# DeltaNet solves in a hybrid decoder trunk: heads stepped by one beat every second row tile, with their matmuls held between two of a projection, and the last residual's transposes held behind one

## The chip, the core and the metric

The kernel runs on one core of a Trainium2 chip. Its engines work side by side, each through its own instructions in the order written for it: TensorE (PE; its weight loads are listed as PEld), VectorE (DVE), ScalarE (ACT), GpSimd (POOL) and SyncE (SP), which here issues most of the transfers. They wait for each other through semaphores. The metric is the device time of one launch in microseconds.

## What is computed

Two decoder layers over 256 tokens of width 2048, all in float32: layer 0 mixes with sparse attention and retention, layer 1 with a gated DeltaNet; each layer then has a cross-attention into 256 memory tokens and a SwiGLU network. The change touches the DeltaNet mixer and the last residual. Cut to what matters:

```python
def gated_deltanet_mixer(h, w_in, conv_w, a_log, dt_bias, norm_gain, w_out):
    qkv, z, b, a = jnp.split(h @ w_in, cuts, axis=-1)
    qkv = jax.nn.silu(causal_depthwise_conv(qkv, conv_w))
    q, k, v = ...                       # 16 query/key heads, 32 value heads of 128
    o = chunk_gated_delta_rule(l2(q), l2(k), v, sigmoid(b), g)
    o = rms_norm(o, norm_gain) * jax.nn.silu(z)
    return o @ w_out

def chunk_gated_delta_rule(q, k, v, beta, g):          # chunks of 64 tokens
    lower = strict(kb @ k.T * decay)
    u, w  = triangular_solve(I + lower, [v * beta, kb * exp(gc)])
    # scan over the chunks:
    v_new = u - w @ state
    o = (q * exp(gc)) @ state + causal(q @ k.T * decay) @ v_new
    state = state * last + k_dec.T @ v_new
```

## The kernel before

Every projection runs as three float32r passes over a high and a low part of its operands (`passes`, L228). A weight tile comes by a SP transfer (L221), ACT makes its high part `w_hi` (L214), DVE the low part `w_lo` (L215), and PE multiplies it into a PSUM tile `pj` (L237, 256 columns a matmul).

Everything else is written as generators ("tasks"). `passes`' callers call `tick()` every six such matmuls, which advances each task that is due; `yield 1` in a task means two ticks, so twelve projection matmuls. This fixes the order in which the program is recorded; a scheduler then fixes the order on each engine, from its own model of durations, and may let instructions pass one another. A held instruction (`tc.issue_after(x)`) may not pass `x`.

In the DeltaNet mixer the sequence is: key and value projections; `invert`, which builds the inverses of all chunk matrices in a tile `AB` and writes them to DRAM as `d_T` by four stores issued from ACT (L1362); the last group of query projections, `queries(3)`; then for g = 0 to 7 a value projection and the solves of four heads, and last the output projection of `o`. A query group is convolved (`cv`: ACT L1061, then three DVE instructions L1063 for each 128 channels), passed through SiLU (`dq`, ACT L1067), and for each of its four heads turned (PE L386), squared and summed (`junk`, ACT L389), scored against the keys (`qk`, PE L1071 and L1072) and copied out (`R`, ACT L1254).

A solve (`pair`, L1394, for two heads; `head`, L1417, for one) takes a PSUM bank of the four in `psg`; the query heads use the same four. `pair` loads blocks of inverses `bd` (L1404) and a row of decays `gb` (L1410). The pool of these tiles lies on the memory of `AB`, so they wait until the four stores have landed. `head` then makes

- `M` and `At`: three DVE instructions (L1422 to L1424, from `gb`), an ACT exponential (L1425), two DVE products (L1426, L1427);
- the value head turned by two PE transposes (L1437) and scaled out as `bv` by two ACT copies (L1441);
- matmuls L1444 and ACT copy `nT` (L1446), then for the two row tiles L1455, DVE L1456, L1458, ACT copy `u` (L1459), with L1452 and DVE L1453 between the tiles;
- the outputs, L1461 to L1463, their sums of squares on ACT (L1467), two POOL instructions (L1468, L1469), three on DVE (L1470, L1472 twice, into `nT`);
- two transposes of `nT` (L1477), and the ACT copy into `R` (L1481) that frees the bank for the next head.

Each head is a task of its own and steps on when it is due; the pace between its steps is `HOP`. The value projection of group g starts when the heads of group g-2 have been turned (`turned`). ACT later splits `o` from `R` (L1013, with DVE and POOL L1014).

## Time and profile before

| | before |
|---|---|
| median of 3 runs | 3003.91 us (3001.68 to 3008.66) |
| the profiled run | 3001.64 us |
| its span in the trace | 2999.8 us, mean granted clock of PE 0.997 |
| PE busy | 2957.6 us, 99% of the span |
| DVE, ACT, POOL busy | 2033.3, 1703.5, 110.3 us |
| solves in the trace | about 1754 to 2077 us |

The span is the traced part; the run is 1.8 us longer. "Busy" of PE counts a matmul from its start to a modelled end, and successive matmuls overlap. PEclk is the share of full speed (2.4 GHz) that PE's clock was granted, 0.5 being 1.2 GHz. An idle time in square brackets stands before its instruction, with the engine and line that ended it. Two transposes or one matmul of 128 columns in plain float32 make two records.

### The profile page before, as it was taken

Reading aid. Unit: us, or ns where it says so; the run is one execution under the profiler, and the core shown is the slowest. Engines: PE = TensorE matmul, PEld = TensorE weight load, DVE = VectorE, ACT = ScalarE, POOL = GpSimd, SP = SyncE. Lnnn points to the kernel's source line nnn. Section 1 sums busy time; section 2 is a strip of 40 time slices with the busy share of each in tenths; the row PEclk is TensorE's granted clock in tenths of the full one; section 3 lists DMA queues with packets and bytes.
Section 4 is the critical chain, followed back from the end, with each engine's and each line's share of the span. In section 5 each row is a group of like instructions: output and inputs, shape, how many; then the busy total and the mean of one; then the engine's idle time right before and its main releaser. Section 6 shows DMA issues by size and latency. Waiting matters only on the chain.

```text
span 2999.8 us, 59557 instructions
## 1 busy us (share of the span) xinstructions
PE 2957.6 (99%) x22917; PEld 2830.7 (94%) x22917; DVE 2033.3 (68%) x3879; ACT 1703.5 (57%) x3328; POOL 110.3 (4%) x153
## 2 busy tenths in 40 slices
PE   8999999999999999999999989999999999999999
PEld 8989899999999999999978989999999999999887
DVE  6867676776665665557689978886667656655554
ACT  6655655665555554447665657776556555445444
POOL 0000000000000000000110101121000000000000
PEclk9999999999999999999999999999999999999999
DMA  7776555656666665566677676663656666666665
GB/s 237 203 233 178 156 147 176 186 174 195 193 195 193 195 195 193 196 191 187 185 220 230 178 208 178 176 177 127 194 187 182 191 193 194 184 189 183 197 199 166
DMA packets 327641, 566.97 MB, mean 189 GB/s; under 512 B 41868, under 2 KB 71620, under 8 KB 327100
## 3 DMA queue, kind: packets, MB, share of 16 engines
q1 hardware_dynamic: 321280, 545.02, 61.0%
q10 hardware_dynamic: 3500, 10.33, 1.3%
q0 software_dynamic: 2576, 7.82, 0.9%
q8 instruction: 179, 2.93, 0.4%
q14 instruction: 106, 0.87, 0.1%
HBM read 549.16 MB, written 13.93 MB: 188 GB/s over the span
## 4 chain that ended last, share of the span: by engine, by line
PE 94%; DMA 2%; DVE 2%; ACT 1%; issue 1%; POOL 0%; SPq 0%; ACTq 0%; DVEq 0%; POOLq 0%
PE pj L237 87%; DVE w_lo L215 1%; DMA w<-in_hyb_w_in 1%; DMA d_T<-AB 1%; PE slv L1458 0%; PE slv L1455 0%; PE slv L1444 0%; ACT w_hi L214 0%; DMA w<-in_nsa_cmp_w 0%; DVE xT L424 0%; POOL AB L1350 0%; DVE x_lo L357 0%; DMA mraw<-in_mem 0%; PE slv L1452 0%; PE qk L1071 0%
## 5 line engine op out<-in xcount | busy, mean ns | idle before, releaser
L215 DVE TENSOR_TENSOR w_lo<-w,w_hi 128x512 fp32r<-128x512 f32 x1938 | 1328.0, 691 | 829.9 <-ACT w_hi L214 818.2
L214 ACT ACTIVATE w_hi<-w 128x512 fp32r<-128x512 f32 x1938 | 1215.1, 631 | 1127.5 <-DVE w_lo L215 591.8
L237 PE MATMUL pj<-x_hi,w_hi 128*128 128x256 f32 (+1 forms) x4496 | 1248.4, 280 | 16.0 <-ACT w_hi L214 15.7
L237 PE MATMUL pj<-x_lo,w_hi 128*128 128x256 f32 x4496 | 1244.0, 279 | 0.0
L237 PE MATMUL pj<-x_hi,w_lo 128*128 128x256 f32 (+1 forms) x4496 | 1225.2, 280 | 0.9 <-DVE w_lo L215 0.9
L237 PEld LDWEIGHTS pj<-x_hi,w_hi 128*128 128x128 f32 (+1 forms) x4496 | 848.4, 189 | 19.5 <-ACT w_hi L214 17.4
L237 PEld LDWEIGHTS pj<-x_lo,w_hi 128*128 128x128 f32 x4496 | 845.6, 188 | 0.8
L237 PEld LDWEIGHTS pj<-x_hi,w_lo 128*128 128x128 f32 (+1 forms) x4496 | 831.6, 188 | 3.2 <-DVE w_lo L215 2.3
L237 PE MATMUL pj<-hl,w_hi 128*128 128x256 f32 x704 | 193.7, 276 | 0.0
L237 PE MATMUL pj<-hh,w_hi 128*128 128x256 f32 x704 | 193.6, 276 | 0.0
L237 PE MATMUL pj<-hh,w_lo 128*128 128x256 f32 x704 | 192.4, 276 | 0.0
L237 PE MATMUL pj<-o,w_hi 128*128 128x256 f32 x1024 | 182.4, 281 | 1.3 <-ACT o L1013 1.1
L237 PE MATMUL pj<-w_lo,x_hi 128*128 128x512 f32 (+2 forms) x448 | 172.0, 385 | 2.6 <-DVE w_lo L215 2.3
L237 PE MATMUL pj<-w_hi,x_lo 128*128 128x512 f32 (+2 forms) x448 | 168.0, 376 | 0.0
L237 PEld LDWEIGHTS pj<-o,w_hi 128*128 128x128 f32 x1024 | 155.9, 189 | 2.0 <-ACT o L1013 1.3
L237 PE MATMUL pj<-o,w_lo 128*128 128x256 f32 x512 | 141.6, 281 | 0.0
L237 PE MATMUL pj<-w_hi,x_hi 128*128 128x512 f32 (+2 forms) x448 | 140.5, 380 | 0.5 <-ACT w_hi L214 0.4
L237 PE MATMUL pj<-w_hi,hl 128*128 128x512 f32 x352 | 138.3, 393 | 0.0
L237 PE MATMUL pj<-w_lo,hh 128*128 128x512 f32 x352 | 137.7, 391 | 0.0
L237 PEld LDWEIGHTS pj<-hh,w_hi 128*128 128x128 f32 x704 | 132.1, 188 | 0.0
L237 PEld LDWEIGHTS pj<-hl,w_hi 128*128 128x128 f32 x704 | 132.1, 188 | 0.0
L237 PEld LDWEIGHTS pj<-hh,w_lo 128*128 128x128 f32 x704 | 131.3, 188 | 0.0
(416 smaller groups left out, 3613.1 us busy)
## 6 DMA issues: line engine op xcount, KB each, us to landing
w<-in_ffn_w_in SPq DMA_DIRECT2D x352, 512.0 KB, 4.2
w<-in_gdn_w_in SPq DMA_DIRECT2D x193, 512.0 KB, 4.2
w<-in_ffn_w_out SPq DMA_DIRECT2D x176, 512.0 KB, 3.7
w<-in_hyb_w_in SPq DMA_DIRECT2D x96, 512.0 KB, 3.7
w<-in_gdn_w_out SPq DMA_DIRECT2D x64, 512.0 KB, 4.4
w<-in_xa_wkv SPq DMA_DIRECT2D x32, 512.0 KB, 4.4
w<-in_hyb_w_out SPq DMA_DIRECT2D x32, 512.0 KB, 4.7
w<-in_nsa_cmp_w SPq DMA_DIRECT2D x16, 512.0 KB, 5.0
```

The costliest lines, as they stand in the source:

```text
L214: state["hi"] = S.activation(h, w, AF.Copy)
L215: state["lo"] = V.tensor_sub(l, w, h.bitcast(F32))
L237: PE.matmul(o, s_, m, start=start and j == 0, stop=last and j == 2, skip_group_check=True)
```

## The change

`HOP` goes from 1 to 2. Heads are no longer tasks of their own: a `Head` puts its generator in the list `active`, and one task, `beat()`, advances all of them together, then yields `HOP`. While it does so (`together()`) every instruction is held behind the last projection matmul recorded, and the next projection matmul is held behind the last of the beat's own PE instructions; `passes` keeps the two references. `pair` yields 3 instead of 1 before its heads, and a head's first yield (between `M`, `At` and its turn) is gone. In the last feed-forward network the 32 transposes of the residual (L672 before) are held behind the projection matmul recorded last.

```diff
--- before.py
+++ after.py
@@ -1,5 +1,5 @@
 import math
-from contextlib import ExitStack
+from contextlib import ExitStack, contextmanager, nullcontext
 
 import numpy as np
 
@@ -28,7 +28,7 @@
 
 
 INV_PACE = 142
-HOP = 1
+HOP = 2
 
 
 BUCKET_STARTS = [16, 21, 27, 35, 46, 59, 77, 99, 128, 166, 216]
@@ -229,12 +229,26 @@
             parts += [(h[:, i, :], l[:, i, :]) for i in range(m)]
         return parts
 
+    @contextmanager
+    def together():
+
+        traced = nc.cur_bb.bb.instructions
+        n = len(traced)
+        mm = state["mm"].ins
+        with tc.issue_after(mm):
+            yield
+        own = [i for i in traced[n:] if i.engine == mm.engine]
+        if own:
+            state["after"] = own[-1]
+
     def passes(o, x, w, start, last, x_stationary=False):
 
         (xh, xl), (h, l) = x, w
         pairs = ((xh, h), (xh, l), (xl, h)) if x_stationary else ((h, xh), (h, xl), (l, xh))
         for j, (s_, m) in enumerate(pairs):
-            PE.matmul(o, s_, m, start=start and j == 0, stop=last and j == 2, skip_group_check=True)
+            after = state.pop("after", None)
+            with tc.issue_after(after) if after is not None else nullcontext():
+                state["mm"] = PE.matmul(o, s_, m, start=start and j == 0, stop=last and j == 2, skip_group_check=True)
 
     class Proj:
 
@@ -668,10 +682,11 @@
                         for t in range(2):
                             yield from take(1)
                             p = bank()
-                            for f in range(4):
-                                PE.transpose(
-                                    p[:, f * P : (f + 1) * P], xT[:, b * 4 + f, t * P : (t + 1) * P], ident
-                                )
+                            with tc.issue_after(state["mm"].ins):
+                                for f in range(4):
+                                    PE.transpose(
+                                        p[:, f * P : (f + 1) * P], xT[:, b * 4 + f, t * P : (t + 1) * P], ident
+                                    )
                             S.activation(xt[:, t, b * 512 : (b + 1) * 512], p, AF.Copy)
                             give(1)
                             yield 2
@@ -1391,6 +1406,29 @@
             G.memset(bd, 0.0)
         gcol = small[:, 16:17]
 
+
+        active = []
+        left = [32]
+
+        class Head:
+            def __init__(self, gen):
+                self.gen, self.done = gen, False
+                active.append(self)
+
+        def beat():
+            while left[0]:
+                with together():
+                    for t in list(active):
+                        try:
+                            next(t.gen)
+                        except StopIteration:
+                            t.done = True
+                            active.remove(t)
+                            left[0] -= 1
+                yield HOP
+
+        spawn(beat())
+
         def pair(q, vT, z, before):
 
             if len(before) == 2:
@@ -1408,9 +1446,9 @@
             gb = gs.tile([P, 2, T], F32, tag="gb", name="gb", bufs=2)
             src = d_rows[:, 2, q]
             nc.sync.dma_start(gb, bass.AP(src.tensor, src.offset, [[0, P], [48 * T, 2], [1, T]]))
-            yield 1
+            yield 3
             begun = []
-            hs = [spawn(head(2 * q + j, j, vT[:, j], z, bd, gb, begun)) for j in range(2)]
+            hs = [Head(head(2 * q + j, j, vT[:, j], z, bd, gb, begun)) for j in range(2)]
             while not all(t.done for t in hs):
                 yield 1
 
@@ -1426,7 +1464,6 @@
             V.tensor_mul(at, m, R[:, q, 384:768])
             V.tensor_mul(m, m, R[:, q, 0:384])
             begun.append(h)
-            yield HOP
             b = bank("slv")
             zc = (h % 4) * P
 
```

The instructions of each engine stay the same in kind and number; their order changes, in the DeltaNet mixer and at the transposes of the residual. Line numbers of the changed kernel are 14 to 38 higher (L237 is L251, L386 is L400, L1071 is L1086, L1437 is L1474, L1477 is L1514, L1481 is L1518).

First place: the start of the solves. PE before, where the first heads are turned, in the middle of the projection of `queries(3)`:

```order
L237 MATMUL pj<-x_hi,w_hi 128x256
L237 MATMUL pj<-x_lo,w_hi 128x256
L1437 MATMUL slv<-ident,vT 128x128 x4
L237 MATMUL pj<-x_hi,w_lo 128x256
L237 MATMUL pj<-x_hi,w_hi 128x256
L237 MATMUL pj<-x_lo,w_hi 128x256
```

PE of the changed kernel: the first such transposes stand behind the last projection matmul of `queries(3)` and behind the turns and scores of its four heads, of which this is the last (`qT` and `qk`), and ahead of the first value projection of the loop:

```order
L1087 MATMUL qk<-dq,R 128x128
L400 MATMUL qT<-ident,dq 128x128 x2
L1086 MATMUL qk<-dq,R 128x256
L1087 MATMUL qk<-dq,R 128x128
L1474 MATMUL slv<-ident,vT 128x128 x8
L251 MATMUL pj<-x_hi,w_hi 128x256
```

The four first turns have moved from inside one projection to the gap between two, and so have the query heads' own instructions, which before stand among matmuls of the next projection.

DVE at the same place, before, from the last of the first four heads' `M`:

```order
L1424 TENSOR_SCALAR M<-gb,colD 128x128
L215 TENSOR_TENSOR w_lo<-w,w_hi 128x512
L1426 TENSOR_TENSOR At<-M,R 128x384 x2
L215 TENSOR_TENSOR w_lo<-w,w_hi 128x512
L1426 TENSOR_TENSOR At<-M,R 128x384 x2
L1427 TENSOR_TENSOR M<-M,R 128x384
L215 TENSOR_TENSOR w_lo<-w,w_hi 128x512
L1427 TENSOR_TENSOR M<-M,R 128x384 x2
L215 TENSOR_TENSOR w_lo<-w,w_hi 128x512
L1427 TENSOR_TENSOR M<-M,R 128x384
L1063 SCALAR_TENSOR_TENSOR cv<-pj,cw,cv 128x255
L215 TENSOR_TENSOR w_lo<-w,w_hi 128x512
```

and in the changed kernel:

```order
L1462 TENSOR_SCALAR M<-gb,colD 128x128
L1464 TENSOR_TENSOR At<-M,R 128x384
L1078 SCALAR_TENSOR_TENSOR cv<-pj,cw,cv 128x255
L215 TENSOR_TENSOR w_lo<-w,w_hi 128x512
L1078 SCALAR_TENSOR_TENSOR cv<-pj,cw,cv 128x255
L1464 TENSOR_TENSOR At<-M,R 128x384 x2
L1465 TENSOR_TENSOR M<-M,R 128x384
L1464 TENSOR_TENSOR At<-M,R 128x384
L1078 SCALAR_TENSOR_TENSOR cv<-pj,cw,cv 128x254 x2
L1465 TENSOR_TENSOR M<-M,R 128x384 x3
L1078 SCALAR_TENSOR_TENSOR cv<-pj,cw,cv 128x253 x2
L1078 SCALAR_TENSOR_TENSOR cv<-pj,cw,cv 128x255 x2
```

Of the changed kernel's rows the convolutions of `queries(3)` (`cv`) stand between the products of the heads and hold all its channels; before, they come after them, mixed with the weights of the next projection.

Second place: the end of a group of four heads, which recurs. PE before, from the second group's end:

```order
L237 MATMUL pj<-x_lo,w_hi 128x256
L237 MATMUL pj<-x_hi,w_hi 128x256
L237 MATMUL pj<-x_lo,w_hi 128x256
L1437 MATMUL slv<-ident,vT 128x128 x2
L1477 MATMUL slv<-ident,nT 128x128 x2
L237 MATMUL pj<-x_hi,w_lo 128x256
L237 MATMUL pj<-x_hi,w_hi 128x256
L237 MATMUL pj<-x_lo,w_hi 128x256
L237 MATMUL pj<-x_hi,w_lo 128x256 x2
L237 MATMUL pj<-x_hi,w_hi 128x256
L237 MATMUL pj<-x_lo,w_hi 128x256
L237 MATMUL pj<-x_hi,w_lo 128x256
```

PE of the changed kernel at the end of the first group; in front of these rows stand 22 projection matmuls, and in front of those the outputs of all four heads (L1498 to L1500):

```order
L251 MATMUL pj<-x_hi,w_lo 128x256
L1514 MATMUL slv<-ident,nT 128x128 x2
L1474 MATMUL slv<-ident,vT 128x128 x2
L1514 MATMUL slv<-ident,nT 128x128 x2
L1474 MATMUL slv<-ident,vT 128x128 x2
L1514 MATMUL slv<-ident,nT 128x128 x2
L1474 MATMUL slv<-ident,vT 128x128 x2
L1514 MATMUL slv<-ident,nT 128x128 x2
L1474 MATMUL slv<-ident,vT 128x128 x2
L251 MATMUL pj<-x_hi,w_hi 128x256
```

The turns of the ending heads (`nT`) and of the beginning ones (`vT`) stand alternately in one piece; this is so at five of the group ends. At the sixth eight turns of `nT`, 48 matmuls of the output projection and eight turns of `vT` follow each other.

ACT before, at such a place:

```order
L1481 ACTIVATE R<-slv,small 128x256
L214 ACTIVATE w_hi<-w 128x512
L1441 ACTIVATE bv<-slv,beta 128x128 x2
L1481 ACTIVATE R<-slv,small 128x256
L214 ACTIVATE w_hi<-w 128x512
L1446 ACTIVATE nT<-slv 128x256
L1481 ACTIVATE R<-slv,small 128x256
L1441 ACTIVATE bv<-slv,beta 128x128 x2
L214 ACTIVATE w_hi<-w 128x512
L1481 ACTIVATE R<-slv,small 128x256
L1441 ACTIVATE bv<-slv,beta 128x128 x2
L214 ACTIVATE w_hi<-w 128x512
```

ACT of the changed kernel:

```order
L1076 ACTIVATE cv<-pj,cw 128x256
L1518 ACTIVATE R<-slv,small 128x256
L1478 ACTIVATE bv<-slv,beta 128x128 x2
L1518 ACTIVATE R<-slv,small 128x256
L1478 ACTIVATE bv<-slv,beta 128x128 x2
L1518 ACTIVATE R<-slv,small 128x256
L1478 ACTIVATE bv<-slv,beta 128x128 x2
L1518 ACTIVATE R<-slv,small 128x256
L1076 ACTIVATE cv<-pj,cw 128x256 x2
```

The copies `R` and `bv` stand alternately, without splits of weights or copies of `nT` between them.

## Rows read from the trace of the kernel before

**Rows 1.** The page's chain of work that ended last, by line.
```profile
PE pj L237 87%; DVE w_lo L215 1%; DMA w<-in_hyb_w_in 1%; DMA d_T<-AB 1%; PE slv L1458 0%; PE slv L1455 0%; PE slv L1444 0%; ACT w_hi L214 0%; DMA w<-in_nsa_cmp_w 0%; DVE xT L424 0%; POOL AB L1350 0%; DVE x_lo L357 0%; DMA mraw<-in_mem 0%; PE slv L1452 0%; PE qk L1071 0%
```

**Rows 2.** Windows: stretch, length, then busy time (instructions) of each engine, PEclk, DMA.
```profile
1754.00:1830.00 76.00, 64.39 (x524) 64.00 (x524) 52.56 (x127) 44.64 (x98) 6.35 (x10) 0.91 0.83 215
1830.00:2085.00 255.00, 250.50 (x2134) 247.41 (x2133) 207.91 (x508) 182.16 (x500) 50.67 (x68) 0.99 0.57 158
...
2500.00:2900.00 400.00, 400.00 (x2806) 373.38 (x2805) 227.35 (x362) 198.14 (x319) 0.00 (x0) 1.00 0.63 191
```

**Rows 3.** All waits of PE: line, releaser, us in total, times, longest.
```profile
PE pj L237 <- ACT w_hi L214: 16.1, 7, 7.6
...
PE slv L1477 <- DVE nT L1472: 2.9, 4, 0.9
```

**Rows 4.** PE in order of time: start, duration, line, operation, count, [idle before <-releaser].
```profile
1754.51 0.60 PE L1437 MATMUL slv<-ident,vT 128*128 128x128 f32 x4
...
1755.07 0.28 PE L237 MATMUL pj<-x_hi,w_hi 128*128 128x256 f32 x1
```

**Rows 5.** ACT and its queue (ACTq) around the four d_T stores.
```profile
1764.56 4.49 ACTq L1362 DMA_DIRECT2D d_T<-AB  x2
1769.14 1.15 ACT L214 ACTIVATE w_hi<-w 128x512 fp32r<-128x512 f32 x2 [6.37 <-issue]
```

**Rows 6.** ACT when the first heads' bv copies run.
```profile
1784.71 2.18 ACT L1441 ACTIVATE bv<-slv,beta 128x128 f32<-128x128 f32 x8 [7.74 <-DMA d_T<-AB]
```

**Rows 7.** PE at the same time.
```profile
1787.46 0.58 PE L237 MATMUL pj<-x_hi,w_hi 128*128 128x256 f32 x1 [7.58 <-ACT w_hi L214]
```

**Rows 8.** Short windows after PE's three long stops; PEclk is the last but two.
```profile
1770.00:1773.00 3.00, 3.00 (x15) 3.00 (x16) 3.00 (x7) 2.06 (x5) 0.00 (x0) 0.54 1.33 311
...
1788.00:1794.00 6.00, 6.00 (x33) 6.00 (x32) 5.06 (x16) 2.80 (x5) 0.00 (x0) 0.56 0.81 160
...
2073.00:2077.00 4.00, 3.71 (x17) 3.49 (x18) 3.38 (x3) 4.00 (x9) 3.17 (x3) 0.57 0.01 2
```

**Rows 9.** The gb loads, all sixteen: time to landing.
```profile
DMA to landing us min/median/max: 4.6/5.8/9.2
```

**Rows 10.** ACT at the first convolution of the last query group.
```profile
1798.64 0.47 ACT L1061 ACTIVATE cv<-pj,cw 128x256 f32<-128x256 f32 x1 [0.59 <-PE pj L237]
```

**Rows 11.** DVE as the first four heads begin.
```profile
1791.48 0.35 DVE L1422 SCALAR_TENSOR_TENSOR M<-gb,colD,cg 128x128 f32<-128x128 f32 x1
...
1792.21 0.34 DVE L1422 SCALAR_TENSOR_TENSOR M<-gb,colD,cg 128x128 f32<-128x128 f32 x1
...
1796.82 1.03 DVE L1426 TENSOR_TENSOR At<-M,R 128x384 f32<-128x384 f32 x2
...
1804.08 0.87 DVE L1063 SCALAR_TENSOR_TENSOR cv<-pj,cw,cv 128x254 f32<-128x254 f32 x2
```

**Rows 12.** ACT at an earlier group of queries: dq, squares and score copies.
```profile
1681.33 0.62 ACT L1067 ACTIVATE dq<-cv 128x512 f32<-128x512 f32 x1
...
1683.11 0.28 ACT L389 ACTIVATE junk<-qT 128x128 f32<-128x128 f32 x1
...
1684.15 0.27 ACT L389 ACTIVATE junk<-qT 128x128 f32<-128x128 f32 x1
```

**Rows 13.** PE in the solves' last stretch, no projection left to run.
```profile
2065.77 0.49 PE L1461 MATMUL slv<-u,At 128*128 128x128 f32 x2
...
2069.65 0.44 PE L1477 MATMUL slv<-ident,nT 128*128 128x128 f32 x2 [0.87 <-DVE nT L1472]
2070.71 0.44 PE L1477 MATMUL slv<-ident,nT 128*128 128x128 f32 x2 [0.62 <-DVE nT L1472]
```

**Rows 14.** ACT in the same stretch.
```profile
2057.86 0.47 ACT L1481 ACTIVATE R<-slv,small 128x256 f32<-128x256 f32 x1 [0.72 <-DVE nT L1472]
2058.23 0.62 ACT L1441 ACTIVATE bv<-slv,beta 128x128 f32<-128x128 f32 x2
2058.73 0.48 ACT L1481 ACTIVATE R<-slv,small 128x256 f32<-128x256 f32 x1
```

## The prediction, made before the changed kernel ran

> **What bounds the kernel now.** I read the chain that ended last first: PE's projection line alone is 87% of it [rows 1], so what counts is where PE stands still. The windows show that it hardly ever does: it is full in the last network, loses 11.6 us of 76 where the solves begin and 4.5 us of 255 while the other solves run [rows 2]. The list of PE's waits then says for what: 16.1 us in seven waits for `w_hi`, and 2.9 us for the solves' `nT` [rows 3]. The other engines have no time that counts of its own; they matter where PE waits for them.
>
> Followed in order of time, the solves hold three long stops of PE. (1) ACT issues the four stores and for 6.37 us splits no weight [rows 5]; PE's share of this is some 4.3 us. (2) The first heads' `bv` copies stand in ACT's order and wait 7.74 us for those stores, because their tiles lie on `AB`; the weight splits queue behind them and PE stands 7.58 us [rows 6, 7]. (3) At the end the projection has run out and PE waits for `nT` of one head after the other, 1.06 us apart [rows 13]. After each stop the clock was granted at 0.54 to 0.57, so at the lower of its levels, 1.2 GHz for most of the window [rows 8]: 3 x 0.46 + 6 x 0.44 + 4 x 0.43 = 5.7 us lost.
>
> **What grouping can save: nothing by itself.** Four transposes and the next projection matmul start within 0.56 us, 0.112 each, which is also the projection's own spacing [rows 4]. Scattered solve matmuls cost no more than grouped ones, so the term is 0. In the middle of a solve the steps now stand 24 projection matmuls apart, 24 x 0.112 = 2.7 us, which covers a DVE or ACT answer of 0.3 to 0.6 us: 0 as well. The second part of the change, 32 transposes of the residual, is moved within a stretch in which PE is busy for 400 of 400 us [rows 2]; the same instructions take the same 32 x 0.11 us, their copies wait for nobody, and the last stands well before the end: 0. If that cover were gone, one copy would show, under 1 us.
>
> **The start of the solves: +9.1 us.** The order has the last query group's whole tail between two projections, with nothing of PE's to cover it, and on DVE the heads' `M` in front of its convolutions. The step that is late first is `gb`. The stores land at 1784.7 now [rows 6]. The convolutions stand ahead of them on ACT in the new order, so I take 2 us later, 1786.7; `gb` then needs 4.6 to 5.8 us [rows 9]: t0 = 1792. PE will have finished the queries by then: the first convolution follows their last matmul at 1798.6 [rows 10]; without stop 2 and its slow clock (7.6 + 2.6 us), and with 1 us more for the stores, that is 1789.1. From t0 DVE alone has four `M` at 0.73 (2.9), eight products at 0.47 (3.8), twelve convolutions at 0.39 (4.7) and two weight splits at 0.63 (1.3; 512 columns at the products' pace for 384): 12.7 us. The paces are those of rows [rows 11] that follow without a gap: 1792.21 - 1791.48 for three instructions of an `M`, and for a row of two its length less one instruction's own (0.56 and 0.48). SiLU, 0.62, brings the first `dq` to t0 + 13. Four heads follow at 1.04 each, then the last `R` copy and the last two turns, whose bank it frees [rows 12]: 0.4 + 4.2 + 0.6 = 5.2. The value projection starts at t0 + 18.2 = 1810.2. Of the 21.1 us since 1789.1 PE's own instructions fill 4.5 (32 records' worth of 128 columns for the query heads and 8 turns, at 0.112). That leaves a stop of 16.6, in place of 7.6: +9. Below: stores not later, `gb` at its quickest, +5; above: `gb` at its slowest 9.2 us, +12.5. Stop (1) itself grows by the two convolution copies and the split that now stand between and ahead of the stores: +1 (0 to 2).
>
> **Five group ends: +23.** Now the sequence on PE is 24 records of outputs, 22 projection matmuls, then `nT`, `vT`, `nT`, `vT` ... From the first output of a head to its `nT` turn the chain over ACT, POOL and DVE took 3.9 us in the last stretch (2065.77 to 2069.65) [rows 13]; the 46 instructions in front take 5.2, so the first turn is not late. But the `vT` turn waits for the `R` copy of the same bank, and the next `R` copy stands on ACT behind the `bv` copies, which wait for the `vT` turn. That is one circle per head: two turns until the copy can start 0.44 [rows 13], `R` 0.47, `bv` pair 0.62 [rows 14], about 1.5 us. PE goes on at 5.2 + 4 x 1.5 + 0.4 = 11.6. Its own work to that point is 24 + 22 + 16 = 62 instructions, 7.0 us: 4.6 us lost each, 23 in all. Nobody else can fill it, since the next projection matmul is held behind the last turn; weights pile up unused meanwhile. Before, the same turns stand apart among matmuls, and 2.9 us of waits for `nT` is all that they cost [rows 3]. Below: copies run without waiting for PE, `R` to `R` 0.87 [rows 14], 2.1 each, 10.5; above: the 1.06 us spacing of `nT` [rows 13] and two convolution copies of 0.47 [rows 10] in the way as well, 6.5 each, 32.
>
> **The sixth end and the last stretch: +2.** At the sixth end the `nT` turns and then the output projection wait, the latter for `R` and its split; I price it like one of the others and, with the turns apart, take +4 (0 to 6.5). At the very end fewer steps are left without cover: the new order keeps one column of matmuls and the eight `nT` turns there. I take -2 of the 4.5 us.
>
> **The clock: +5.** Each stop of the old solves was followed by a window at the lower level, worth 1.4 to 2.6 us [rows 8], the one of the last stretch with PE busy part of the time in front. The new ends are of that kind: turns, 1.5 us apart, for 6 us. I take it for three of five at 1.7; 0 to 11 is open.
>
> Sum: 9 + 1 + 23 + 4 - 2 + 5 = +40 us on the profiled run's 3001.6, so 3041.7; the median of the runs lies 2.3 above the profiled one, so **3044 us**. The bounds add up to +13.5 (3017) and +64 (3068).
>
> **A rule that would make it worse.** The Trainium skill, page "TensorE: Matmul & The Clock Gate", section "A second HAM failure mode: psum-queue depth-cycling", says that a PE which idles briefly between groups of matmuls while it cycles through PSUM banks swings between half and full clock and pays the return each time. By that rule all five ends and the sixth would be paid for. The trace agrees as far as it goes: the last stretch, the only place of this form, is followed by a window at 0.57 [rows 8].
>
> **Rivals.**
> - *The clock falls at every end.* Six windows at up to 2.6 us, 15 instead of 5, and the start and ends toward their upper bounds: +50 to +64, 3052 to 3068. For it: all three old stops did so. Against: the ends are shorter than stops 2 and 3.
> - *The ends stay cheap.* If ACT runs `R` and `bv` without waiting for PE, the ends cost 10 or less and their clock nothing; the start remains: +13 to +25, 3017 to 3029. For it: the 0.87 us spacing [rows 14]. Against: those rows belong to different banks, while the new order alternates strictly.
> - *Faster.* The mechanism is stop 2: `bv` no longer stands ahead of the weight splits while the stores are under way, so its 7.6 us and the 2.6 us of slow clock behind it disappear, 10 us, down to 2993. It decides if all new stops together stay under 4 us. That needs `gb` landed by the time the queries end, 2.4 us after its issue, against 4.6 at best [rows 9], and ends under 0.8 us, against 2.1 at their lower bound.
> - *No difference*, within 6 us (0.2%, about what a measurement of this kernel can tell from no change): the held order costs about what stop 2 gave back, the ends nearly hidden.
>
> **Chances.** The forecast, 3029 to 3052: 0.58. Ends cheap 0.18; clock at every end 0.15; no difference 0.05; faster 0.04. So slower 0.91, same 0.05, faster 0.04. The range that leaves out the tails of the outer cases is 3015 to 3064.
>
> **What would show it.** In the new trace PE should stand some 15 us at one place before the first value projection, with a DVE chain of `M`, products and `cv` as what ended the wait, and no long `bv` wait for the stores ahead of weight splits. At five places, some 37 us apart (192 projection matmuls, 96 records of the solves and the stop), the two transposing lines should alternate 1.5 us apart, with waits for `R` on ACT, of 4 to 5 us in sum each, and often a stretch at half clock after it. The window of the last network should be unchanged. I am wrong if PE's idle time in the solves is not some 30 us above before, if the time is lost in the middle of solves (then 24 matmuls are no cover), or if it shows in the last network (then the transposes were not free).

## The result, and the profile after

| | before | after |
|---|---|---|
| median | 3002.80 us (4 runs, 3000.77 to 3008.66) | 3049.04 us (4 runs, 3047.43 to 3055.04) |
| ratio to before, 95% interval | | 1.0152 (1.0140 to 1.0164) |
| span of the profiled run | 2999.8 us | 3053.3 us, mean granted clock 0.988 |

Of before there is one run more here than ahead of the prediction. The changed kernel is 46.2 us slower; 3044 was forecast, with 3015 to 3064 as its range. The profiled run of after is the longest of the four, 6.0 us above their median; the traces differ by 53.5 us, and the terms below are read from them. Line numbers are those of the changed kernel.

The waits of PE, as [rows 3] (line, releaser, us in total, times, longest):

```profile
PE pj L251 <- ACT w_hi L214: 15.3, 7, 9.3
PE slv L1474 <- ACT R L1518: 13.9, 20, 0.9
PE qT L400 <- ACT dq L1082: 13.0, 1, 13.0
PE slv L1514 <- DVE nT L1509: 11.3, 13, 3.4
```

Three of these four are new or four times as long: one stop for the query heads, twenty for `R`, thirteen for `nT`. The first is as long as before, and was expected to lose its longest member. The windows of the same stretches, as [rows 2] and [rows 8]:

```profile
1754.00:1820.00 66.00, 41.38 (x322) 39.91 (x321) 35.58 (x80) 32.52 (x73) 5.28 (x5) 0.82 0.69 189
1820.00:2135.00 315.00, 287.43 (x2292) 276.38 (x2291) 221.86 (x552) 198.78 (x521) 46.36 (x72) 0.93 0.48 140
...
1854.34:1857.35 3.01, 3.01 (x16) 3.01 (x15) 2.64 (x7) 1.83 (x5) 0.00 (x0) 0.50 0.40 150
1893.93:1898.31 4.38, 4.38 (x22) 4.38 (x21) 4.01 (x9) 2.63 (x6) 0.00 (x0) 0.50 0.32 118
1934.08:1939.27 5.19, 5.19 (x26) 5.19 (x25) 4.33 (x9) 2.64 (x6) 0.00 (x0) 0.50 0.30 110
1974.43:1976.82 2.39, 2.39 (x13) 2.39 (x12) 2.39 (x6) 1.22 (x4) 0.00 (x0) 0.50 0.76 241
2013.85:2017.78 3.93, 3.93 (x20) 3.93 (x19) 3.28 (x8) 2.48 (x6) 0.00 (x0) 0.50 0.43 140
2055.11:2058.74 3.63, 3.63 (x19) 3.63 (x18) 3.44 (x8) 1.72 (x4) 0.00 (x0) 0.50 0.52 150
```

PE stands still for 24.6 of 66 us where the solves begin and for 27.6 of 315 in the rest of them, 52.2 us in all against 16.1 before. Behind each of the five group ends and behind the sixth (the last six rows) the granted clock, PEclk (last but two), is 0.50: PE works at 1.2 GHz there for 22.5 us in sum.

**The start.** PE in order of time:

```profile
1769.95 0.39 PE L251 MATMUL pj<-x_hi,w_hi 128*128 128x256 f32 x1 [2.29 <-ACT w_hi L214]
...
1789.38 0.58 PE L251 MATMUL pj<-x_hi,w_hi 128*128 128x256 f32 x1 [9.35 <-ACT w_hi L214]
...
1809.56 0.69 PE L400 MATMUL qT<-ident,dq 128*128 128x128 f32 x2 [12.98 <-ACT dq L1082]
```

The stop behind the stores' issue is 2.29 in place of 4.3 us. The second, 9.35, is there although no `bv` copy stands in front of the weight splits any more. ACT shows who is late, and what later lies ahead of the query heads:

```profile
1788.70 1.15 ACT L214 ACTIVATE w_hi<-w 128x512 fp32r<-128x512 f32 x2 [12.91 <-DMA w<-in_gdn_w_in]
...
1807.58 1.28 ACT L1082 ACT_TABLE_LOAD   x1 [1.76 <-DVE cv L1078]
1808.87 1.15 ACT L1082 ACTIVATE dq<-cv 128x512 f32<-128x512 f32 x2
```

The split waits 12.91 us for its own weight tile. In the new trace the four weight loads issued behind the stores, from 1770.65 on, take 15.6 to 17.9 us from issue to landing. The kernel before already had this. Its three loads there take 12.6 to 14.7 us; this is the first of them, issued at 1771.13:

```profile
L221 SPq DMA_DIRECT2D w<-in_gdn_w_in x1: 367/367/367, 1771.1 to 1771.1; - x1
...
DMA to landing us min/median/max: 14.7/14.7/14.7
```

It landed at 1785.8, 1.1 us behind the stores (1784.7) and 0.9 us before ACT had finished the `bv` copies and split it at 1786.7. So without `bv` in front that stop would have been some 0.9 us shorter, and not 7.6. In the changed kernel the stores land 2.5 us later, at 1787.2, when `gb` is issued, and the weight tile at 1788.6. The query heads' wait is the chain forecast, on DVE:

```profile
1795.05 0.35 DVE L1460 SCALAR_TENSOR_TENSOR M<-gb,colD,cg 128x128 f32<-128x128 f32 x1
...
1805.46 2.43 DVE L1078 SCALAR_TENSOR_TENSOR cv<-pj,cw,cv 128x255 f32<-128x255 f32 x6 [0.15 <-ACT cv L1076]
```

From the first `M` to the end of the last convolution are 1807.89 - 1795.05 = 12.84 us; 12.7 was summed.

**A group end.** PE at the first of the five:

```profile
1846.99 0.28 PE L251 MATMUL pj<-x_hi,w_lo 128*128 128x256 f32 x1
1847.42 0.44 PE L1514 MATMUL slv<-ident,nT 128*128 128x128 f32 x2
1848.61 0.44 PE L1474 MATMUL slv<-ident,vT 128*128 128x128 f32 x2 [0.75 <-ACT R L1518]
1849.47 0.44 PE L1514 MATMUL slv<-ident,nT 128*128 128x128 f32 x2 [0.42 <-DVE nT L1509]
1850.47 0.67 PE L1474 MATMUL slv<-ident,vT 128*128 128x128 f32 x2 [0.56 <-ACT R L1518]
...
1854.00 0.69 PE L1474 MATMUL slv<-ident,vT 128*128 128x128 f32 x2 [0.66 <-ACT R L1518]
1854.34 0.56 PE L251 MATMUL pj<-x_hi,w_hi 128*128 128x256 f32 x1
```

and ACT beside it:

```profile
1848.09 0.46 ACT L1518 ACTIVATE R<-slv,small 128x256 f32<-128x256 f32 x1
1849.08 0.63 ACT L1478 ACTIVATE bv<-slv,beta 128x128 f32<-128x128 f32 x2 [0.53 <-PE slv L1474]
1849.94 0.47 ACT L1518 ACTIVATE R<-slv,small 128x256 f32<-128x256 f32 x1 [0.23 <-PE slv L1514]
1851.18 0.63 ACT L1478 ACTIVATE bv<-slv,beta 128x128 f32<-128x128 f32 x2 [0.76 <-PE slv L1474]
```

This is the circle of the prediction: PE's `vT` turn waits for `R`, ACT's `bv` for the `vT` turn, one head after the other. From 1846.99 to 1854.34 are 7.35 us for 17 starts; at 0.112 they would take 1.9. Of the 5.4 lost, 0.7 are turns that run at half clock. The five ends lose 5.4, 5.2, 5.0, 5.0 and 5.2 us, 25.8 in all; without turns at half clock, some 2.2 us, it is 23.6, or 4.7 each. The sixth end, where eight splits of `o` stand on ACT in between:

```profile
2047.19 0.44 PE L1514 MATMUL slv<-ident,nT 128*128 128x128 f32 x2
2049.23 0.44 PE L1514 MATMUL slv<-ident,nT 128*128 128x128 f32 x2 [1.60 <-DVE nT L1509]
2050.94 0.44 PE L1514 MATMUL slv<-ident,nT 128*128 128x128 f32 x2 [1.27 <-DVE nT L1509]
2054.77 0.69 PE L1514 MATMUL slv<-ident,nT 128*128 128x128 f32 x2 [3.40 <-DVE nT L1509]
```

**The sum.** Behind the last head's turn PE goes on with the output projection at 2129.10, and before at 2073.29, 55.8 us later, with 6910 of its records left in both. The end is 53.5 later, so behind the solves after is 2.3 us quicker. Of the 55.8, the start has 2.29 - 4.3 = -2, 9.35 - 7.58 = +1.8 and +13.0, the five ends 23.6, the sixth 7.1, the last stretch one more wait of 0.6: 44.1 in all. The remaining 11.7 us are the clock, as an estimate from rows shows. At 0.50 projection matmuls start 0.214 us apart (1854.70 to 1857.05 are eleven steps), at 1.00 0.113, so a stretch at 0.50 loses 0.47 of its length: 10.6 us of the 22.5 behind the six ends, and 1.6 of the 3.42 us from 1809.56 to 1812.98, at the query heads. The turns inside the ends add the 2.2 us from above. Against that stand the stretches at 0.50 behind the first two stops, 9.0 us before (1769.6 to 1772.8 and 1787.5 to 1793.3) and 3.1 after (1789.4 to 1792.5): -2.8. The sum is 11.6. In which of these terms the 6.0 us lie by which this run is above the median, no row tells.

### The profile page after: what moved, and what is told of

Its sections match the earlier page's. It is cut to its first block, busy times and chain, and to the rows that moved or that the text cites. A ratio compares the mean times of both kernels' runs of the same rounds, so it can differ in the third digit from the quotient of the medians.

```text
span 3053.3 us, 59597 instructions
## 1 busy us (share of the span) xinstructions
PE 2974.5 (97%) x22917; PEld 2838.8 (93%) x22917; DVE 2034.4 (67%) x3879; ACT 1712.4 (56%) x3328; POOL 105.9 (3%) x153
## 5 line engine op out<-in xcount | busy, mean ns | idle before, releaser
L251 PE MATMUL pj<-x_hi,w_hi 128*128 128x256 f32 (+1 forms) x4496 | 1251.0, 281 | 15.3 <-ACT w_hi L214 14.9
L251 PE MATMUL pj<-x_lo,w_hi 128*128 128x256 f32 x4496 | 1241.4, 279 | 0.0
L251 PE MATMUL pj<-x_hi,w_lo 128*128 128x256 f32 (+1 forms) x4496 | 1218.6, 279 | 0.9 <-DVE w_lo L215 0.9
L251 PEld LDWEIGHTS pj<-x_hi,w_hi 128*128 128x128 f32 (+1 forms) x4496 | 849.4, 189 | 18.7 <-ACT w_hi L214 16.5
L251 PEld LDWEIGHTS pj<-x_lo,w_hi 128*128 128x128 f32 x4496 | 849.1, 189 | 0.8
L251 PEld LDWEIGHTS pj<-x_hi,w_lo 128*128 128x128 f32 (+1 forms) x4496 | 834.0, 189 | 3.4 <-DVE w_lo L215 2.5
L251 PE MATMUL pj<-hl,w_hi 128*128 128x256 f32 x704 | 193.7, 276 | 0.0
L251 PE MATMUL pj<-hh,w_hi 128*128 128x256 f32 x704 | 193.6, 276 | 0.0
L251 PE MATMUL pj<-hh,w_lo 128*128 128x256 f32 x704 | 192.4, 276 | 0.0
L251 PE MATMUL pj<-o,w_hi 128*128 128x256 f32 x1024 | 186.5, 286 | 1.1 <-ACT o L1028 1.1
L251 PE MATMUL pj<-w_lo,x_hi 128*128 128x512 f32 (+2 forms) x448 | 172.2, 386 | 2.9 <-DVE w_lo L215 2.6
L251 PE MATMUL pj<-w_hi,x_lo 128*128 128x512 f32 (+2 forms) x448 | 168.2, 376 | 0.0
L251 PEld LDWEIGHTS pj<-o,w_hi 128*128 128x128 f32 x1024 | 158.8, 192 | 1.7 <-ACT o L1028 1.5
L251 PE MATMUL pj<-o,w_lo 128*128 128x256 f32 x512 | 143.1, 284 | 0.2 <-DVE w_lo L215 0.2
L251 PE MATMUL pj<-w_hi,x_hi 128*128 128x512 f32 (+2 forms) x448 | 140.1, 379 | 0.5 <-ACT w_hi L214 0.4
L251 PE MATMUL pj<-w_lo,hh 128*128 128x512 f32 x352 | 138.9, 395 | 0.0
L251 PE MATMUL pj<-w_hi,hl 128*128 128x512 f32 x352 | 137.7, 391 | 0.0
L251 PEld LDWEIGHTS pj<-hl,w_hi 128*128 128x128 f32 x704 | 132.1, 188 | 0.0
L251 PEld LDWEIGHTS pj<-hh,w_hi 128*128 128x128 f32 x704 | 132.1, 188 | 0.0
L251 PEld LDWEIGHTS pj<-hh,w_lo 128*128 128x128 f32 x704 | 131.3, 188 | 0.0
```

The costliest lines, as they stand in the source:

```text
L251: state["mm"] = PE.matmul(o, s_, m, start=start and j == 0, stop=last and j == 2, skip_group_check=True)
```

## The experiments

Theory A came from the trace: what costs the time is that the next projection matmul is held behind each beat, so that PE has nothing to run when a step waits. The ratios are to the kernel before, measured beside it on the same chip; runs taken once have no interval.

**Without the hold behind** (the first hold, in front, stays):

```diff
-        own = [i for i in traced[n:] if i.engine == mm.engine]
-        if own:
-            state["after"] = own[-1]
```

> The changed kernel without the second hold: the next projection matmul is no longer held behind the beat; the first hold, HOP 2 and the beat stay. Theory A (the time is lost because the order forced on PE leaves the group ends and the queries' tail without projection matmuls beside them): the turns stand among projection matmuls again, PE's idle time in the solves goes back from about 64 us to about 20, and the run takes 2998 to 3010 us. Rival B (stepping four heads together every 24 matmuls costs by itself): 3030 us or more. Rival C (the loss is mostly the slower clock after each stop): the clock goes back with the stops, so the same time as A; the split between idle time and clock is read from this run's windows.

Measured: 3003.89 us (10 runs), ratio 1.0005 (0.9996 to 1.0014). Theory A holds: this hold is worth 45 us. Some 5 of them are lost behind the solves, where PE is always busy: the 2000 PE records behind the last head take 241.3 us in the changed kernel, 236.3 here and 235.3 before (on the pace, see below). Rival C's clock is 11.7 of the 55.8 us in the sum above, so a part and not most. The query stop is gone, and so are the five ends with all but one of their `R` waits; the stop for weights stays, at 10.3 us.

**Ends without the hold.** After a beat that holds a head's `vT` or `nT` turn nothing is held, except for the first four heads:

```diff
-        if own:
+        if own and not state.pop("turns", False):
             state["after"] = own[-1]
...
+            if h > 3:
+                state["turns"] = True
             for t in range(2):
                 PE.transpose(b[:, 256 + t * P : 256 + (t + 1) * P], vT[:, t * P : (t + 1) * P], ident)
...
             yield 2 * HOP
+            state["turns"] = True
```

> The changed kernel without the second hold in the beats that turn nT at a group's end or vT of the next heads; the first four heads' turns and all other beats stay held. Theory A (the circle of turn, R copy, turn, bv copy at six ends makes 30 us of idle time and most of the clock loss): the waits of the nT and vT turns, 25 us in the changed kernel, fall under 5, the 13 us stop ahead of the queries' turns stays, and the run takes 3008 to 3020 us. Rival B (the held steps in the middle of solves matter as much): 3030 us or more.

Measured: 3016.06 us (5 runs), ratio 1.0045 (1.0030 to 1.0060). PE's waits from 1740 to 2160:

```profile
PE qT L400 <- ACT dq L1082: 12.6, 1, 12.6
PE pj L251 <- ACT w_hi L214: 11.4, 2, 10.2
PE slv L1517 <- DVE nT L1511: 4.2, 6, 1.3
```

The ends, the sixth included, are worth 33 us with their clock and with the same 5 us behind the solves (236.5 us here for the 2000 records). What is left above the run without the hold, 12.2 us, is about the query stop of 12.6.

**The query stop alone:**

```diff
-            yield 3
+            yield 1
             begun = []
```

> The changed kernel with the pair's yield before its heads back at 1 (3 in the change), so the first heads begin inside the last query projection and the queries' tail falls among the first heads' steps. Theory A: the 13.3 us stop ahead of the query turns goes, the stop of 9 to 10 us behind the stores stays (bv waits there again, or the weights), the group ends stay at 4.7 us each: 3030 to 3038 us. Rival B: no difference to the changed kernel, 3044 to 3054.

Measured: 3039.39 us (4 runs), ratio 1.0124 (1.0109 to 1.0139), 9.7 us under the changed kernel and a little above the expectation. The wait for `dq` is gone, the ends are there (`R` 11.4 us in 16 waits, `nT` 11.0 in 12).

**Beats twice as often:**

```diff
-HOP = 2
+HOP = 1
```

> The changed kernel with HOP 1: beats every 12 projection matmuls instead of 24. A group of four heads then takes less than one projection, so its end falls inside a projection. Theory A: the start stays as slow as in the changed kernel, the five ends lose about 2 us each instead of 4.7 (the nT turns still wait for POOL), some clock comes back: 3028 to 3038 us. Rival B (the held beats themselves cost; with twice as many per projection matmul the waits inside the solves grow): 3049 us or more.

Measured: 3061.43 us (4 runs), ratio 1.0201 (1.0185 to 1.0216). Theory A's number missed by more than 20 us; the rival's came. PE's waits from 1740 to 2160:

```profile
PE pj L251 <- DVE w_lo L215: 15.0, 11, 2.6
PE qT L400 <- ACT dq L1082: 12.9, 1, 12.9
PE pj L251 <- ACT w_hi L214: 12.0, 4, 7.8
PE slv L1514 <- DVE nT L1509: 6.9, 12, 3.2
PE slv L1474 <- DVE vT L414: 4.6, 4, 1.5
```

The circle of `R` and `bv` is gone, but PE now waits eleven times for the low part of a weight and four times for `vT`, the value projection's own convolution, and still 6.9 us for `nT`. So the ends don't depend on the circle alone: at the narrower pace the held order waits at other steps, and longer.

**Each store twice.** `d_T` is also written to a second scratch tensor that nobody reads:

```diff
-            S.dma_start(
-                d_T[j].rearrange("r i w j -> r (i w j)"), AB[32 * j : 32 * j + 32].rearrange("p i w j -> p (i w j)")
-            )
+            for d in (d_T[j], state["d_T2"][j]):
+                S.dma_start(
+                    d.rearrange("r i w j -> r (i w j)"), AB[32 * j : 32 * j + 32].rearrange("p i w j -> p (i w j)")
+                )
```

> The changed kernel with each of the four stores of the inverses issued twice, the second time to a DRAM tile that nothing reads: 8.4 MB instead of 4.2. Theory T (the second stop is the weights' transfers, slowed by the stores): the stop of 9.4 us grows by 8 us or more with the weights' transfer as what ACT waits for, and with gb later the run is 10 to 25 us above the changed kernel. Rival (the stop has another cause): the second stop stays within 3 us of 9.4.

Measured: 3065.98 us (one run), 16.9 above the changed kernel. ACT at the second stop:

```profile
1806.01 1.15 ACT L214 ACTIVATE w_hi<-w 128x512 fp32r<-128x512 f32 x2 [21.99 <-DMA w<-in_gdn_w_in]
```

The split's wait grew from 12.91 to 21.99 us and PE's stop from 9.35 to 17.79. The first stop grew too, from 2.29 to 12.40, as ACT issues eight stores there. So the weight transfers are late behind the stores' bytes; that `bv` stood in front was no cause that could be taken away. In the traces of before, after and six of these runs the first weight tile behind the stores lands 0.7 to 1.5 us after the last store.

**The residual's transposes alone**, on the solves of before:

```diff
-                            for f in range(4):
+                            with tc.issue_after(state["mm"].ins):
+                                for f in range(4):
```

> The kernel before with only the last part of the change: the residual's 32 transposes held behind the projection matmul recorded last. Theory A: no difference, 2999 to 3008 us, PE full from 2500 to 2900 us. Rival: the copies come late for the last additions and the end grows by 1 to 5 us.

Measured: 2993.73 us (10 runs), ratio 0.9971 (0.9962 to 0.9981): 9 us faster where no difference was expected. Windows of the kernel before, and then of this one:

```profile
2450.00:2530.00 80.00, 80.00 (x708) 80.00 (x707) 48.69 (x81) 40.63 (x67) 0.00 (x0) 1.00 0.66 192
2540.00:2620.00 80.00, 80.00 (x682) 80.00 (x681) 47.05 (x79) 39.49 (x64) 0.00 (x0) 1.00 0.65 186
```
```profile
2540.00:2620.00 80.00, 80.00 (x708) 80.00 (x707) 49.79 (x84) 41.44 (x67) 0.00 (x0) 1.00 0.62 195
```

PE is busy for 80 of 80 us at a granted clock of 1.00 in each of them, and yet does 708 matmuls in one and 682 in the other: 0.113 and 0.117 us for each. The kernel before has one residual transpose between two projection matmuls at 2531.74, and from there on the slower pace, up to about 2750; its next transposes come at 2756.5. Held, all 32 stand at 2739 to 2762, so none comes there. 218 us at 26 in 708 are 8.0 us, about what was gained.

**What sets the pace.** On top of that kernel, five tasks in the last network each put transposes of the identity, whose result nobody uses, between two projection matmuls: 1, 1, 2, 3, 4 of them in one run, 1, 6, 2, 3, 5 in the other.

```diff
+                def extra(n):
+                    yield 5
+                    yield from take(1)
+                    p = bank()
+                    with tc.issue_after(state["mm"].ins):
+                        for f in range(n):
+                            state["after"] = PE.transpose(p[:, f * P : (f + 1) * P], ident, ident).ins
...
+                    if last and b in (1, 3, 5, 7, 9):
+                        spawn(extra({1: 1, 3: 1, 5: 2, 7: 3, 9: 4}[b]))
```

> The kernel before with the residual's transposes held (as in e2_tail) and with 1, 1, 2, 3 and 4 extra transposes of the identity put between two projection matmuls at five places of the last network's input projection, 85 us apart; their results go to a scratch tile, the output is unchanged. Theory P (a projection runs at one of two paces, 0.113 or 0.118 us a matmul, and a lone transpose between two of its matmuls switches it): 0.113 up to the first, 0.118 after the first, 0.113 again after the second; after 2, 3 and 4 the pace says which numbers switch it (those of 3 did not in the kernel before, those of 4 not in e2_tail). Rival Q (the slow pace came from the transposes that waited for a bank, or from where the program stood): 0.113 throughout.

> As e14_extra, with 1, 6, 2, 3 and 5 extra transposes. Theory P3 (a multiple of three, the length of the projection's own cycle of passes, gives the fast pace, any other number the slow one): 0.118 after 1, 0.113 after 6, 0.118 after 2, 0.113 after 3, 0.118 after 5. Rival (three alone is special, or the number does not decide): 0.118 after 6.

Measured: 3008.18 and 3003.14 us (one run each). Windows of the first, between its groups:

```profile
2320.00:2400.00 80.00, 80.00 (x681) 80.00 (x681) 46.79 (x78) 38.71 (x64) 0.00 (x0) 1.00 0.59 185
...
2590.00:2670.00 80.00, 80.00 (x709) 80.00 (x708) 48.51 (x81) 40.98 (x67) 0.00 (x0) 1.00 0.61 193
2680.00:2735.00 55.00, 55.00 (x469) 55.00 (x469) 32.19 (x55) 27.01 (x44) 0.00 (x0) 1.00 0.60 189
```

and of the second:

```profile
2410.00:2490.00 80.00, 80.00 (x682) 80.00 (x681) 45.53 (x76) 39.24 (x63) 0.00 (x0) 1.00 0.66 187
2500.00:2580.00 80.00, 80.00 (x708) 80.00 (x707) 48.43 (x81) 40.45 (x66) 0.00 (x0) 1.00 0.68 192
...
2680.00:2735.00 55.00, 55.00 (x488) 55.00 (x487) 33.36 (x56) 29.91 (x48) 0.00 (x0) 1.00 0.68 193
```

It is shown that transposes put in between switch the pace, in both directions, and that it then stays until the next ones. It was slow after one, one again, two and four of them, and fast after three in the first run; slow after one and six, fast after two, three and five in the second. So both theories failed: the second single transpose did not bring back the fast pace, six left it slow and five fast. The number alone does not decide it, since two gave both. Nor does PE's order alone: in the changed kernel and in the run with each store twice PE's last 9242 records, from the start of the solves on, have the same order, tiles and shapes, and in the 80 us from 2140 the one has 682 of them, in the 80 us from 2160 the other 709. What does decide was not found.

**Three transposes where the pace was slow anyway**, at layer 0's output projection (the same task with 3, on the kernel with the held residual):

```diff
+        if h == 3:
+            spawn(extra(3))
```

> The kernel of e2_tail with three extra transposes of the identity (into a scratch tile) held together between two matmuls of layer 0's output projection, behind the last transposes of the retention heads, where the pace falls from 0.113 to 0.118 us a matmul for about 98 us. Theory P3 (after three, the pace is the fast one, whatever it was): 0.113 from there on, 4 us less than e2_tail, 2987 to 2992 us, in which the three cost 0.3. Rival: the fast pace after three in the last network was chance of that place: no gain, 2993 to 2996.

Measured: 2994.55 us (6 runs), ratio 0.9961 (0.9949 to 0.9973). From 500 to 580 us 708 matmuls ran in place of 681, the fast pace, but the interval overlaps that of the kernel without them and the 2987 to 2992 us of the theory did not come: whether 3 us were gained in the whole can't be told. In the trace, the slowest of the six runs, the gain is lost again behind the solves, where the 2000 records take 240.6 us in place of 235.9, at the slow pace (682 from 2090 to 2170, and 708 without the three).

**Stores issued from POOL**, with the held residual, so that ACT goes on splitting weights:

```diff
-            S.dma_start(
+            G.dma_start(
```

> The kernel of e2_tail with the four stores of the inverses issued from POOL instead of ACT. If ACT's 6.4 us of issuing make the first stop of the solves, that stop (4.3 us) goes and the run is 4 to 6 us faster than e2_tail: 2987 to 2991 us. If the weights' transfers behind the stores make the second stop, it stays at 7 us or more. Rival: POOL's way of issuing is slower, the stores land later and the second stop grows by what the first gives: no difference to e2_tail, 2990 to 2997.

Measured: 2997.13 us (10 runs), ratio 0.9982 (0.9972 to 0.9991). The first stop is gone, but the second grows to 13.2 us; there too ACT's split waits for its weight tile:

```profile
1785.93 0.63 ACT L214 ACTIVATE w_hi<-w 128x512 fp32r<-128x512 f32 x1 [15.74 <-DMA w<-in_gdn_w_in]
```

The rival's outcome came, no difference that can be told from the held residual alone (2993.73 us, with intervals that overlap). The two stops look like one shortage of weights: without the first, PE has used up sooner what was at hand, and waits longer in the second.

**Neither hold, but the beat**, in place of both holds of `together()` a plain `yield`:

```diff
-        with tc.issue_after(mm):
-            yield
-        own = [i for i in traced[n:] if i.engine == mm.engine]
-        if own:
-            state["after"] = own[-1]
+        yield
```

> The changed kernel without either hold of its solve steps: heads still step by the one beat every second row tile, their instructions may pass and be passed by projection matmuls; the residual's transposes keep their hold. With only the hold behind removed the kernel ran at 3003.9 us, while the held residual transposes alone, on the solves of before, ran at 2993.7: 10.2 us still lie in the beat, the later turn of a pair, and the hold in front. Theory F (the hold in front costs them): without it 2990 to 2997 us. Rival G (the beat itself costs them, because a slower step lets the sixth end and the last stretch run into each other and stop 2 grow): no difference from 3003.9, 3000 to 3008 us, PE's w_hi stop of 10 us and at least 5 us more idle between 1980 and 2090 than with the solves of before.

Measured: 3001.82 us (12 runs), ratio 0.9997 (0.9987 to 1.0007). Rival G's time came; by the medians the hold in front costs 2 us, which the intervals do not tell from nothing. The beat costs some 8 us against the solves of before (0.9997 against 0.9971). G's places are right for the stop, 9.9 us, and small for the end: PE is busy for 101.67 us between 1980 and 2090, and for 105.50 before, 3.8 us less and not 5.

## Why the prediction was right

The forecast of a slower kernel was right, by the mechanisms that it named for the largest terms, and partly by luck, in errors that cancelled. The start is the clearest case: +10 was forecast, -2 + 1.8 + 13.0 = +12.8 came, because what stop 2 did not give back PE did not wait a second time at the query heads. PE's idle time in the solves rose by 36.1 us, where "some 30" was the sign of being right.

| term | forecast | in the trace after |
|---|---|---|
| grouping, middle of the solves | 0 | 0 |
| first stop, at the stores' issue | +1 | -2 |
| second stop | -7.6 | +1.8 |
| query stop | +16.6 | +13.0 |
| five ends | +23 | +23.6 |
| sixth end | +4 | +7.1 |
| last stretch | -2 | +0.6 |
| clock, and the rest | +5 | +11.7 |
| behind the solves | 0 | -2.3 |
| sum | +40 | +53.5 (46.2 between the medians) |

- **Right: the five ends.** Both the circle and its price. The run without the hold at the ends confirms it: no wait for `R` is left, and 33 us go, in which the sixth end, the clock and some 5 us of pace behind the solves are counted.
- **Right: the middle of the solves.** Of the waits inside a solve the trace after has one, 0.4 us for a DVE `bv`; 24 projection matmuls are cover enough.
- **Mis-sized: the first stop**, -2 for +1. A split and a convolution copy do stand between the stores on ACT, but its longest pause for issuing is 4.13 us, where it was 6.37 [rows 5], so weights come sooner and not later.
- **Failed: "without stop 2".** The prediction, and its rival *Faster*, took the `bv` copies on `AB` to be what ends that wait, as [rows 6] names the stores. Behind them the weights themselves were late, in the kernel before too, where the next tile landed 0.9 us before its split: a wait of 12.91 us in the changed kernel, 21.99 with the stores doubled. A queue held by one late transfer hid a second one. The prediction asked of the trace "no long `bv` wait for the stores ahead of weight splits"; there is none, and the stop is there all the same.
- **Mis-sized: the query stop**, +13.0 for 16.6. The DVE chain was right to 0.1 us (12.84 for 12.7). PE came to the queries 7.2 us later than thought, at 1796.3 in place of 1789.1 (its terms add up to 1789.4), since the second stop was still in front; the first `M` came at 1795.05, 3 us later than the 1792 of the sum. Not in the sum was ACT's table load of 1.28 us, of which 0.97 stand open between the convolutions and `dq`. Counted as the prediction counts, up to the value projection at 1815.74 and less 4.5 us of PE's own work, the stop is some 15 us; the part behind the wait is mostly the clock, and stands in that row of the table.
- **Mis-sized: the sixth end**, +7.1 for 4: eight splits of `o`, 4.26 us on ACT, stand between the `R` copies there, and the turns wait for them up to 3.40 us. **The last stretch** keeps its waits, 0.62 us each, and has one more.
- **Mis-sized: the clock**, 11.7 for 5. The prediction took three of five ends; behind all five and the sixth PEclk is 0.50, for 2.4 to 5.2 us each. So the mechanism of the rival *The clock falls at every end* came, to which 0.15 was given; its time, 3052 to 3068, did not, for the median. The rule of the Trainium skill that stood against the change (page "TensorE: Matmul & The Clock Gate", section "A second HAM failure mode: psum-queue depth-cycling", told there of bf16 matmuls of 512 columns) has the return paid at each such place, and the trace agrees with it.
- **Failed: the residual's transposes at 0**, "the same instructions take the same 32 x 0.11 us". The transposes cost what was said; the projection matmuls behind one of them ran at 0.117 in place of 0.113 us for 218 us. Alone, this part makes the kernel 9 us faster. In the changed kernel it is mostly not to be seen, because PE runs at the slow pace behind the solves: from 2140 to 2220 the trace after has 682 matmuls, the one before 705, and the 2000 records behind the last head take 6.0 us more. Why is open; the new order of the solves is not enough for it, since the run with each store twice has that order and the fast pace there.

By experiments the change is: the hold behind, +45; the beat, about +8; the hold in front, nothing that can be told; the residual's hold, -9. Of the 45 some 5 are the pace behind the solves. The residual's hold alone is the quickest kernel of the study beside the one with three transposes more.

## What to carry to other kernels

Holding filler work behind a step, so that a group stays together, takes away the work that hides the step's wait; price each place at which two engines then answer each other in turn, and the clock behind it. When a wait is to vanish, ask which transfer the next instruction in that queue needs and when that one lands. A stretch in which an engine is busy all the time has still a pace: count instructions per microsecond on both sides of an edit.

## What was not expected of the hardware

Back-to-back projection matmuls of 256 columns run at one of two paces, 0.113 or 0.117 us, both at a granted clock of 1.00 and with PE busy throughout. Other PE instructions put in between can switch from one to the other, and it then held until the next of them, in the kernel before for 218 us. The same order of instructions on PE ran at either pace in two runs (682 and 709 in 80 us). What selects the pace stays open.
